# State-space layouts in DRAM, the products of the taps a step behind, and the rotary tables loaded earlier

## The chip, the core and the metric

The kernel runs on one core of a Trainium2 chip. The metric is device time in microseconds (us). Five engines run at the same time and are tied by semaphores: PE (matrix products; PEld, its weight load, lies beside it), DVE and ACT (element by element), POOL (here small additions, memsets and DMA issues) and SP (DMA issues only). Each engine takes its instructions in the order of the program.

## What is computed

The reference is a hybrid decoder block for one sequence of 512 rows, to which 16 learned rows are prepended (528 in all), width 2048. On the same RMS-normalised input run an attention with compressed queries and keys, and a diagonal complex state-space layer of 64 groups of 16 channels with 64 states each. The two are merged by gates; an output projection and a SwiGLU feed-forward layer follow.

```python
n = rms_norm(h, norm_mix[l])
z = n @ w_in[l]
q_lat, kv_lat, k_r, u, gates = jnp.split(z, [OFF_Q, OFF_KV, OFF_KR, OFF_U], axis=-1)
q = rms_norm(q_lat, norm_q[l]) @ w_q_up[l]          # 16 heads, 128 + 64 (rotary)
kv = rms_norm(kv_lat, norm_kv[l]) @ w_kv_up[l]
attn_out = mla_attention(q_nope, q_rope, k_nope, k_rope, v) @ w_attn_proj[l]
# state space: x_t = a x_(t-1) + b u_t,  y_t = Re(c x_t) + d u_t, per group
y = s5_scan(u.reshape(bsz, length, SSM_GROUPS, SSM_GROUP), lam_re, lam_im, log_step, b, c, d)
y = jax.nn.gelu(y)
ssm_out = (y @ w_glu_val[l]) * jax.nn.sigmoid(y @ w_glu_gate[l])
mixed = jax.nn.sigmoid(g0) * attn_out + jax.nn.sigmoid(g1) * ssm_out
h = h + mixed @ w_out[l]
h = h + (jax.nn.silu(m @ w_ffn_gate[l]) * (m @ w_ffn_up[l])) @ w_ffn_down[l]
out = rms_norm(h, norm_final)[:, N_META:]
```

## The kernel before

**Products and weights.** All is float32. A product with weights is made of three products of halves: weight and activation are each split into a high and a low half. Weights come in blocks of 8 tiles of 128 x 128 (512 KB). The class `Weights` streams them: SP loads a block into `raw`, ACT copies it to its high half `whi` (L262), DVE subtracts to get the low half `wlo` (L263), and a ring of three of each is kept ahead of PE. `st.use()` takes the next block. PE's instructions are nearly all at L316, inside `mm`; DVE's additions and products of two tiles are at L323 (`tt`), so groups are told apart by their tiles.

**Background work.** The program is written out by hand: the order of the calls is the order on each engine. Behind each block of weights a hook, `bg()`, lets generators in the background go on by a budget of time, at each of their `yield`s. So the work of the state-space layer is laid between the blocks of the projections: `ssm_first` beside the projections of u, q, kv (what the prediction calls the table stage), `ssm_main` and `x_products` beside the attention projection (the scan stage).

**The state-space layer.** The sequence is taken in 66 chunks (NC_) of 8 rows (CL), the 64 groups in four batches `b` of 16 groups (BG), a batch as 8 pairs (BP). u leaves the first projection transposed, one tile of 128 channels at a time: `evac_u` scales a tile on DVE and POOL stores it to `ud` (L871). `ssm_params` loads the parameters `sprm` (L519) and makes powers of the poles on DVE. Then, for each of the four batches, one after the other:

- `ssm_tables`: loads `sw` and `sK` (L669, L671); ACT copies C (through `C48`) and the first 18 columns of the powers `rt` into `ER`, DVE doubles these to 66 columns, POOL stores them to `ed` (L686). DVE expands the table BL in `ssA` (two halves of three operations of 128x1024). PE multiplies BL with C48 into the bank Q of the PSUM (psQ): these are the products of the tables, the taps of the filter; DVE adds them to `sK`, and eight stores of POOL take them to `kd` (L699). PE transposes BL in four groups (psB, L705), ACT copies them to `ssB` (L706), POOL stores that to `bd` (L708).
- `ssm_powers`: DVE expands the table CL, in the same tile `ssA` as BL, and four stores take it to `cd` (L720).

In `ssm_main` a batch loads BL's transposes (`load_b`, L743), its part of u (`load_u`, L737: eight loads, one for each row of a chunk, gathered in pieces of 264 bytes), the E tables (`load_e`, L748), and the matrix of taps (`load_t`): a memset of `ssB` (L763) and eight loads from `kd` (L766), which lay the taps as a block-Toeplitz matrix of 128 x 128 for each group, then CL (L770). PE makes the states' inputs, DVE scans, PE makes the outputs; `store` takes y to `yd` in eight stores (L823), from which the gates read it in rows of channels.

**Queues.** POOL issues these transfers in order. They take eight semaphores in turn, so that an issue waits for the transfer eight before it. What stands on POOL behind a waiting issue waits too.

**Rotary tables.** `kcs` (L933), the rotary table of the key, is loaded by POOL behind the last projection of kv; `cs` (L947), that of the queries, behind it, in the tile `sC`, which held C.

The loads of u and of the matrix of taps before:

```python
U = sb([P, BG, NC_], F32, ("U", "H0")[b % 2])
for i in range(CL):
    POOL.dma_start(U[i * 16:(i + 1) * 16],
                   ud[g0 * 16:(g0 + BG) * 16, CL - 1 - i].rearrange("(g p) c -> p g c", p=16))
```

## Time and profile before

| | before |
|---|---|
| time, median of 3 runs | 2859.46 us (2857.26 to 2861.65) |
| the profiled execution's own time | 2853.81 us |
| its span | 2852.0 us |
| mean granted clock of PE | 0.982 |
| PE busy | 2756.4 us, 97% of the span |
| PEld busy | 2601.1 us, 91% |
| DVE busy | 2047.4 us, 72% |
| ACT busy | 1222.1 us, 43% |
| POOL busy | 479.1 us, 17% |
| read from and written to DRAM | 342.32 MB and 75.10 MB, 146 GB/s over the span |

The span is the stretch between the first and the last instruction of the profiled execution; its own time has a little around it. The page gives the same busy shares in 40 slices of 71.3 us each, in tenths, and under them the clock granted to PE:

```profile
PE   9977999997899999999999999999999999999997
...
DVE  7866666655367777343468888888888888788896
...
POOL 2222211046420001111122000000000003030112
PEclk9988999998999999999999999999999999999999
DMA  5444222188664444544443433334333337474542
```

PE is below nine tenths in the third and fourth slices (143 to 285 us) and in the tenth and eleventh (642 to 784 us), and at the very end. Where PE waits, its clock is below full as well. The rows that the text below quotes from groups of instructions read: line, engine, operation, tile out <- tiles in, count, then busy us and mean ns of one, then the idle time before them and what ended most of it. Rows of the timeline begin with the time in us from the span's start and the duration, and end with the wait before them in brackets. Rows of stretches have the window, its length, then busy us and instructions of PE, PEld, DVE, ACT and POOL, then PE's granted clock, the busy share of the DMA engines, and GB/s.

### The profile page before, as it was taken

The numbers are of one execution on the slowest core, as the hardware profiler recorded it, in microseconds if no ns is written. First come the engines' busy times: TensorE is split into PE (matmuls) and PEld (weight loads), VectorE is DVE, ScalarE is ACT, GpSimd is POOL, SyncE is SP. The second block draws the span as 40 slices with busy tenths as digits, with TensorE's granted clock in tenths as the row PEclk, the third lists the DMA queues.
The fourth block names the chain that finished last, engine by engine and source line by source line (L and its number), as shares of the span: only waits on it lengthen the run. The fifth ranks groups of instructions, "written<-read, shape, count | busy, mean of one in ns | idle before, by whom it ended". The sixth has DMA issues, their size and how long they took to land.

```text
span 2852.0 us, 50236 instructions
## 1 busy us (share of the span) xinstructions
PE 2756.4 (97%) x20782; PEld 2601.1 (91%) x20782; DVE 2047.4 (72%) x2682; ACT 1222.1 (43%) x1774; POOL 479.1 (17%) x729
## 2 busy tenths in 40 slices
PE   9977999997899999999999999999999999999997
PEld 8876999976789999888889999999999999999997
DVE  7866666655367777343468888888888888788896
ACT  5222555532254445222234444444444445354445
POOL 2222211046420001111122000000000003030112
PEclk9988999998999999999999999999999999999999
DMA  5444222188664444544443433334333337474542
GB/s 190 143 130 119 82 67 67 49 243 260 190 251 148 137 150 143 162 138 144 135 138 126 148 126 126 133 134 141 127 133 129 138 127 258 162 266 157 196 166 97
DMA packets 126628, 426.38 MB, mean 149 GB/s; under 512 B 18208, under 2 KB 23008, under 8 KB 125312
## 3 DMA queue, kind: packets, MB, share of 16 engines
q1 hardware_dynamic: 76672, 263.36, 27.3%
q0 software_dynamic: 48944, 158.71, 17.3%
q8 instruction: 163, 2.67, 0.4%
q10 hardware_dynamic: 784, 1.11, 0.1%
q14 instruction: 65, 0.53, 0.1%
HBM read 342.32 MB, written 75.10 MB: 146 GB/s over the span
## 4 chain that ended last, share of the span: by engine, by line
PE 84%; DVE 6%; DMA 4%; issue 3%; POOL 1%; ACT 1%; DVEq 0%; POOLq 0%; ACTq 0%
PE psA L316 48%; PE psB L316 22%; PE psQ L316 6%; PE psV L316 5%; PE psD L316 2%; DVE T L323 1%; DMA ER<-ed 1%; DVE wlo L263 1%; DVE S L323 1%; DVE ev L323 1%; DMA xd<-H 1%; DMA sw<-in_sb 0%; ACT whi L262 0%; PE psA L1124 0%; PE psB L705 0%
## 5 line engine op out<-in xcount | busy, mean ns | idle before, releaser
L316 PE MATMUL psA<-S,whi 128*128 128x256 f32 (+2 forms) x5136 | 1122.9, 309 | 13.1 <-ACT whi L262 6.3
L316 PEld LDWEIGHTS psA<-S,whi 128*128 128x128 f32 x5136 | 843.7, 189 | 68.6 <-ACT whi L262 7.8
L316 PE MATMUL psA<-S,wlo 128*128 128x256 f32 (+2 forms) x2568 | 789.9, 308 | 0.0
L263 DVE TENSOR_TENSOR wlo<-raw,whi 128x1024 fp32r<-128x1024 f32 (+1 forms) x479 | 591.5, 1236 | 193.8 <-ACT whi L262 191.9
L262 ACT ACTIVATE whi<-raw 128x1024 fp32r<-128x1024 f32 (+1 forms) x479 | 504.5, 1055 | 414.8 <-PE psA L316 180.4
L316 PEld LDWEIGHTS psA<-S,wlo 128*128 128x128 f32 x2568 | 485.1, 189 | 26.0
L263 DVE TENSOR_TENSOR wlo<-cmb,whi 128x1024 fp32r<-128x1024 f32 x225 | 274.9, 1222 | 96.2 <-ACT whi L262 95.2
L316 PE MATMUL psB<-S,whi 128*128 128x256 f32 (+1 forms) x1632 | 330.1, 284 | 1.1 <-ACT ssB L706 0.9
L262 ACT ACTIVATE whi<-cmb 128x1024 fp32r<-128x1024 f32 x225 | 237.7, 1056 | 202.5 <-DVE wlo L263 142.0
L316 PEld LDWEIGHTS psB<-S,whi 128*128 128x128 f32 x1632 | 265.6, 190 | 2.4 <-ACT ssB L706 1.8
L316 PE MATMUL psB<-S,wlo 128*128 128x256 f32 (+1 forms) x816 | 230.3, 282 | 0.0
L316 PEld LDWEIGHTS psB<-S,wlo 128*128 128x128 f32 x816 | 154.6, 189 | 0.0
L1332 POOL DMA_DIRECT2D td<-sC x22 | 15.8, 718 | 764.4 <-ACT ev L1251 718.1
L316 PE MATMUL psA<-H,whi 128*128 128x512 f32 (+2 forms) x448 | 120.6, 356 | 11.4 <-DVE S L323 6.1
L316 PEld LDWEIGHTS psA<-H,whi 128*128 128x128 f32 x448 | 78.5, 194 | 22.3 <-issue 6.6
L243 DVE TENSOR_TENSOR cmb<-raw,raw 128x1024 f32<-128x1024 f32 x75 | 91.4, 1218 | 6.1 <-DMA raw<-in_wst 5.1
L323 DVE TENSOR_TENSOR H<-H,psA 128x256 f32<-128x256 f32 (+1 forms) x42 | 22.5, 535 | 96.8 <-POOL H L323 88.0
L243 DVE TENSOR_TENSOR cmb<-cmb,raw 128x1024 f32<-128x1024 f32 x75 | 91.4, 1219 | 0.0
L243 DVE TENSOR_TENSOR raw<-raw,raw 128x1024 f32<-128x1024 f32 x75 | 91.3, 1218 | 0.0
L243 DVE TENSOR_TENSOR cmb<-raw,cmb 128x1024 f32<-128x1024 f32 x75 | 91.3, 1217 | 0.0
L1251 ACT ACTIVATE ev<-psA 128x256 f32<-128x256 f32 x114 | 43.5, 381 | 100.8 <-PE psA L316 100.6
L316 PE MATMUL psA<-H,wlo 128*128 128x512 f32 (+2 forms) x224 | 78.3, 350 | 0.0
(675 smaller groups left out, 5461.7 us busy)
## 6 DMA issues: line engine op xcount, KB each, us to landing
raw<-in_wst SPq DMA_DIRECT2D x485, 512.0 KB, 3.7
td<-sC POOLq DMA_DIRECT2D x22, 512.0 KB, 3.2
td<-H POOLq DMA_DIRECT2D x40, 256.0 KB, 3.3
S<-td POOLq DMA_DIRECT2D x40, 256.0 KB, 7.1
H<-sg POOLq DMA_DIRECT2D x16, 512.0 KB, 4.0
bd<-ssB POOLq DMA_DIRECT2D x4, 1024.0 KB, 4.2
...
```

Source lines behind the costliest of these rows:

```text
L243: self.nc.vector.tensor_tensor(t, g(a), g(b), op=op)
L262: self.nc.scalar.activation(hi[:, a:b], w[:, a:b], AF.Copy)
L263: self.nc.vector.tensor_tensor(lo[:, a:b], w[:, a:b], hi[:, a:b], op=ALU.subtract)
L316: PE.matmul(o, lhsT=l, rhs=r, start=start, stop=stop, skip_group_check=more)
L323: eng.tensor_tensor(o, a, b, op=op)
L1251: ACT.activation(snap[name], o, AF.Copy)
L1332: POOL.dma_start(dst[0:2].rearrange("f p n -> p f n"), pair)
```

## The change

Five things are changed.

1. **u in DRAM.** `ud` is laid out as a batch takes it, [4, 128, 16, 66]. `evac_u` reverses the rows of a chunk and issues eight stores of 16 partitions (one for each group of the tile) instead of one; `load_u` is one load instead of eight.
2. **The matrix of taps in DRAM.** It is put together once, in the table stage, by a new function `toeplitz`, and stored whole to `wt` (1 MB for each batch); `load_t` is one load instead of a memset and eight loads.
3. **Order of the table stage.** `ssm_first` now holds the whole loop. CL is expanded right behind BL and has a tile of its own (the tag `ER`; the E tables went to `H7`). The products of the taps stand behind CL, go to the bank D, and are added and taken to `kd` a step later, by `toeplitz(*behind)`; the last one comes behind a `yield 5`. The powers `rt` lose their column of ones (17 instead of 18), C shares their tiles and is loaded earlier; CL is stored in two transfers instead of four.
4. **y in DRAM.** `store` is one store to `yt`; 32 copies from DRAM to DRAM (`y_rows`), four in each of eight tiles of the gates, lay the rows out in `yd`.
5. **Rotary tables.** `cs` is loaded before the projections of kv instead of behind them (its tile `sC` no longer holds C). `kcs` stays where it is.

```diff
-    ud = dp.tile([1024, CL, NC_], F32, name="ud")
+    ud = dp.tile([4, P, BG, NC_], F32, name="ud")
+    yt = dp.tile([4, P, BG, 64], F32, name="yt")
     yd = dp.tile([1024, CL, 64], F32, name="yd")
     kd = dp.tile([16, 64, CL, 16], F32, name="kd")
+    wt = dp.tile([4, P, BG * P], F32, name="wt")
...
         v = lambda t: t[:, :n_ * k].rearrange("p (a b) -> p a b", b=k)
-        bc = lambda t: t[:, :, m:m + 1].to_broadcast([P, n_, k])
-        cmul(e[0][:, :, m + 1:m + 1 + k], e[1][:, :, m + 1:m + 1 + k], e[0][:, :, 1:1 + k], e[1][:, :, 1:1 + k],
-             bc(e[0]), bc(e[1]), v(T1), v(T2))
+        bc = lambda t: t[:, :, m - 1:m].to_broadcast([P, n_, k])
+        cmul(e[0][:, :, m:m + k], e[1][:, :, m:m + k], e[0][:, :, :k], e[1][:, :, :k], bc(e[0]), bc(e[1]),
+             v(T1), v(T2))
...
-        rt = [sb([P, 32, 18], F32, t) for t in ("v", "w")]
-        tabs["rt"] = rt
-        POOL.memset(rt[0][:, :, 0], 1.0)
-        POOL.memset(rt[1][:, :, 0], 0.0)
+        vw = [sb([P, 2 * T], F32, t) for t in ("v", "w")]
+        rt = [t[:, :544].rearrange("p (j c) -> p j c", c=17) for t in vw]
+        C = [t[:, 544:].rearrange("p (j q) -> p j q", q=16) for t in vw]
+        tabs["rt"], tabs["C"] = rt, C
         for i in range(2):
-            DVE.tensor_copy(rt[i][:, :, 1], e8[:, i])
+            POOL.dma_start(C[i], A["sc"][:, i])
+            DVE.tensor_copy(rt[i][:, :, 0], e8[:, i])
         yield 0.4
         for m, k in ((1, 1), (2, 2), (4, 4), (8, 8), (16, 1)):
             double(rt, m, k, 32, T1, T2)
             yield 0.8 + 0.2 * k
 
-        C = sb([P, 2, 32, 16], F32, "sC")
-        tabs["C"] = C
-        POOL.dma_start(C, A["sc"])
         tabs["C48"] = sb([P, 2, BP, 48], F32, "U")
         POOL.memset(tabs["C48"], 0.0)
...
-    def ssm_tables(b):
...
-        ER = sb([P, 2, BP, NC_], F32, "ER")
-        for i in range(2):
-            ACT.activation(ER[:, i, :, :18], tabs["rt"][i][:, js], AF.Copy)
-        yield 0.3
-        for m, k in ((17, 17), (34, 31)):
-            double((ER[:, 0], ER[:, 1]), m, k, BP, T1, T2)
-            yield 1.0 + 0.05 * k
-        POOL.dma_start(ed[b], ER.rearrange("p a j c -> p a (j c)"))
-        BL = sb([P, 2, BP, CL * 16], F32, "ssA")
-        yield from expand(BL, Bt, js, 0, 1, T1, T2)
-        yield 1
-        pk = ps([P, 512], "Q")
-        for j in range(BP):
-            for i in range(2):
-                for r in RH:
-                    mm(pk[r, j * 32:(j + 1) * 32], BL[:, i, j, r], C48[:, i, j, 16:48], i == 0, i == 1)
-        tt(Dg, pk[:, :BG * 16], Dg, ADD)
-        for i in range(CL):
-            POOL.dma_start(kd[:, g0:g0 + BG, i], Dg[i * 16:(i + 1) * 16].rearrange("p (g o) -> p g o", o=16))
...
-    def ssm_powers(b):
-        js = slice(b * BP, (b + 1) * BP)
-        C48 = tabs["C48"]
-        CLt = sb([P, 2, BP, P], F32, "ssA")
-        yield from expand(CLt, C48, js, 1, -1, T1, T2)
-        for g in range(2):
-            for r in range(2):
-                POOL.dma_start(cd[b, g, r * 64:(r + 1) * 64],
-                               CLt[g * 64:(g + 1) * 64, r].rearrange("p j m -> p (j m)"))
-    def ssm_first():
-        yield from ssm_params()
-        for b in range(4):
-            yield from ssm_tables(b)
-            yield from ssm_powers(b)
+    def ssm_first():
...
+        def taps(b, BL):
+            pk = ps([P, 2, 512], "D")[:, 0]
+            for j in range(BP):
+                for i in range(2):
+                    for r in RH:
+                        mm(pk[r, j * 32:(j + 1) * 32], BL[:, i, j, r], C48[:, i, j, 16:48], i == 0, i == 1)
+            return pk
+        def transposed(b, BL, BT, j):
             pt = ps([P, 4, P], "B")
             for i in range(4):
                 PE.transpose(pt[:, i], BL[:, i % 2, j + i // 2], ident)
             ACT.activation(BT[:, j:j + 2].rearrange("p a b c -> p (a b) c"), pt, AF.Copy)
+        def toeplitz(b, pk, Dg):
             g0 = b * BG
+            tt(Dg, pk[:, :BG * 16], Dg, ADD)
             for i in range(CL):
+                POOL.dma_start(kd[:, g0:g0 + BG, i], Dg[i * 16:(i + 1) * 16].rearrange("p (g o) -> p g o", o=16))
             TT = sb([P, BG, P], F32, "ssB")
             POOL.memset(TT, 0.0)
             for i in range(CL):
                 s = CL - 1 - i
                 POOL.dma_start(TT[i * 16:(i + 1) * 16, :, s * 16:],
                                kd[:, g0:g0 + BG, 0:i + 1].rearrange("p g t o -> p g (t o)"))
+            POOL.dma_start(wt[b], TT.rearrange("p g m -> p (g m)"))
+        behind = None
+        for b in range(4):
+            js, g0 = slice(b * BP, (b + 1) * BP), b * BG
+            Bt = sb([P, 2, BP, 16], F32, "sw")
+            POOL.dma_start(Bt, A["sb"][:, :, js])
+            Dg = sb([P, BG * 16], F32, "sK", bufs=2)
+            POOL.dma_start(Dg, A["sd"][:, g0 * 16:(g0 + BG) * 16])
+            for ph, c in ((slice(0, P), 0), (RH[0], 16), (RH[1], 32)):
+                for i in range(2):
+                    ACT.activation(C48[ph, i, :, c:c + 16], tabs["C"][i][ph, js], AF.Copy)
+            ER = sb([P, 2, BP, NC_], F32, "H7")
+            POOL.memset(ER[:, 0, :, 0], 1.0)
+            POOL.memset(ER[:, 1, :, 0], 0.0)
+            for i in range(2):
+                ACT.activation(ER[:, i, :, 1:18], tabs["rt"][i][:, js], AF.Copy)
+            yield 0.1
+            for m, k in ((17, 17), (34, 31)):
+                double((ER[:, 0, :, 1:], ER[:, 1, :, 1:]), m, k, BP, T1, T2)
+                yield 1.0 + 0.05 * k
+            POOL.dma_start(ed[b], ER.rearrange("p a j c -> p a (j c)"))
+            if behind:
+                toeplitz(*behind)
+                yield 0.4
+            BL = sb([P, 2, BP, CL * 16], F32, "ssA")
+            yield from expand(BL, Bt, js, 0, 1, T1, T2)
+            CLt = sb([P, 2, BP, P], F32, "ER")
+            yield from expand(CLt, C48, js, 1, -1, T1, T2)
+            for g in range(2):
+                POOL.dma_start(cd[b, g].rearrange("(r s) m -> s r m", r=2),
+                               CLt[g * 64:(g + 1) * 64].rearrange("p r j m -> p r (j m)"))
+            behind = b, taps(b, BL), Dg
+            BT = sb([P, BP, 2, P], F32, "ssB")
+            for j in range(0, BP, 2):
+                transposed(b, BL, BT, j)
+                if j == 2:
+                    yield 0.1
+            POOL.dma_start(bd[b], BT.rearrange("p j a c -> p (j a c)"))
+            yield 0.1
+        yield 5
+        toeplitz(*behind)
...
         def load_u(b):
...
-            for i in range(CL):
-                POOL.dma_start(U[i * 16:(i + 1) * 16],
-                               ud[g0 * 16:(g0 + BG) * 16, CL - 1 - i].rearrange("(g p) c -> p g c", p=16))
+            POOL.dma_start(U, ud[b])
...
         def load_t(b):
             TT = sb([P, BG, P], F32, "ssB")
-            POOL.memset(TT, 0.0)
...
+            POOL.dma_start(TT.rearrange("p g m -> p (g m)"), wt[b])
...
         def store(b):
-            g0, Y = b * BG, nxt_["Y", b]
-            for t in range(CL):
-                POOL.dma_start(yd[g0 * 16:(g0 + BG) * 16, t].rearrange("(g p) c -> p g c", p=16),
-                               Y[t * 16:(t + 1) * 16])
+            POOL.dma_start(yt[b], nxt_["Y", b])
...
     def evac_u(j, outs):
         u = ev()
-        uv = u.rearrange("p (s c) -> p c s", s=CL)
+        uv = u.rearrange("p (s c) -> p c s", s=CL)[:, :, ::-1]
...
-        POOL.dma_start(ud[j * P:(j + 1) * P].rearrange("f s c -> f (s c)"), u)
+        rows = ud[j // 2].rearrange("(i p) g c -> p i g c", p=16)
+        for g in range(8):
+            POOL.dma_start(rows[:, :, j % 2 * 8 + g], u[g * 16:(g + 1) * 16].rearrange("p (i c) -> p i c", i=CL))
...
+    cs = sb([P, 2, SEQ], F32, "sC")
+    POOL.dma_start(cs, A["cs"][:, :, META:])
     acc_kv = sb([P, T], F32, "KS")
...
-    cs = sb([P, 2, SEQ], F32, "sC")
-    POOL.dma_start(cs, A["cs"][:, :, META:])
...
+    def y_rows(b, t):
+        POOL.dma_start(yd[b * BG * 16:(b + 1) * BG * 16, t].rearrange("(g p) c -> p g c", p=16),
+                       yt[b, t * 16:(t + 1) * 16])
...
+        for i in range(4 * j - 8, 4 * j - 4):
+            if 0 <= i < 32:
+                y_rows(i // CL, i % CL)
```

How the order of the instructions moves is shown at three places. A row is the line, the operation, the tile written and the tiles read (with a running number behind the name), and the shape; x8 stands for eight like rows. The lines of the changed kernel are its own.

First POOL near the start, while u is projected. `acc` is the sum of squares of the input, `ud` the stores of u, `sprm` the parameters with which the tables begin. Before:

```order
L323 TENSOR_TENSOR acc_112<-acc_112,ev_384 128x528
L871 DMA ud<-ev_567 128x528
L871 DMA ud<-ev_571 128x528
L871 DMA ud<-ev_575 128x528
L519 DMA sprm_635<-in_sprm 128x96
L871 DMA ud<-ev_726 128x528
```

And the same place with the change:

```order
L323 TENSOR_TENSOR acc_114<-acc_114,ev_386 128x528
L874 DMA ud<-ev_569 16x8x66 x8
L874 DMA ud<-ev_580 16x8x66 x8
L874 DMA ud<-ev_591 16x8x66 x8
L521 DMA sprm_658<-in_sprm 128x96
L874 DMA ud<-ev_749 16x8x66 x8
```

24 transfers instead of three stand ahead of the load of `sprm`.

Second DVE in the third step of the tables (b = 2), where the projection of q ends. `T` and `T_..` are the two terms of an expansion, `ssA` BL, `ev` and `psQ` the norm of q, `wlo` a block of weights. Before, from the first half of BL on:

```order
L323 TENSOR_TENSOR T_132_1857<-sw_1853,spw_184 128x1024
L323 TENSOR_TENSOR T_133_1858<-sw_1853,spw_184 128x1024
L323 TENSOR_TENSOR ssA_1932<-T_132_1857,T_133_1858 128x1024
L332 TENSOR_SCALAR ev_1936<-psQ_1937 128x512
L323 TENSOR_TENSOR ev_1936<-ev_1936,acc_1307 128x512 x2
L332 TENSOR_SCALAR ev_1936<-ev_1936 128x512
L323 TENSOR_TENSOR acc_1307<-acc_1307,ev_1936 128x512
```

With the change, from the second half of BL on (`ER` is CL here, `U` holds C48):

```order
L323 TENSOR_TENSOR T_83_1352<-sw_1849,spw_186 128x1024
L323 TENSOR_TENSOR T_84_1353<-sw_1849,spw_186 128x1024
L323 TENSOR_TENSOR ssA_1961<-T_83_1352,T_84_1353 128x1024
L263 TENSOR_TENSOR wlo_1969<-raw_1729,whi_1968 128x1024
L323 TENSOR_TENSOR T_83_1352<-U_1289,spw_186 128x1024
L323 TENSOR_TENSOR T_84_1353<-U_1289,spw_186 128x1024
L323 TENSOR_TENSOR ER_2022<-T_83_1352,T_84_1353 128x1024
L332 TENSOR_SCALAR ev_2026<-psQ_2027 128x512
```

The norm of q stood between the two halves of BL, ahead of the products; it now stands behind BL and the first half of CL.

Third POOL at the end of the tables (b = 3), up to the load of `kcs` (tile `S`). `KS` is the sum of squares of kv. Before:

```order
L699 DMA kd<-sK_2222 16x16x16 x8
L708 DMA bd<-ssB_2469 128x2048
L323 TENSOR_TENSOR KS_1792<-KS_1792,ev_2504 128x528
L720 DMA cd<-ssA_2497 64x1024 x4
L933 DMA S_196_2656<-in_kcs 128x528
L938 DMA KS_2661<-S_196_2656 64x528
L947 DMA sC_2669<-in_cs 128x2x512
```

With the change, behind `bd` and the addition to `KS`:

```order
L690 DMA kd<-sK_2225 16x16x16 x8
L692 MEMSET ssB_2671 128x2048
L695 DMA ssB_2671<-kd 16x16x16
L695 DMA ssB_2671<-kd 16x16x32
L695 DMA ssB_2671<-kd 16x16x48
L695 DMA ssB_2671<-kd 16x16x64
L695 DMA ssB_2671<-kd 16x16x80
L695 DMA ssB_2671<-kd 16x16x96
L695 DMA ssB_2671<-kd 16x16x112
L695 DMA ssB_2671<-kd 16x2048
L697 DMA wt<-ssB_2671 128x2048
L938 DMA S_186_2756<-in_kcs 128x528
```

The stores to `kd`, the memset, the eight loads of the matrix and its store now stand right ahead of the load of `kcs`.

More of the change, by code (lines that the diff above doesn't have):

```diff
@@ L627, in ssm_params @@
             yield 0.8 + 0.2 * k
-        C = sb([P, 2, 32, 16], F32, "sC")
-        tabs["C"] = C
-        POOL.dma_start(C, A["sc"])
         tabs["C48"] = sb([P, 2, BP, 48], F32, "U")
         POOL.memset(tabs["C48"], 0.0)
-        yield 3.6
         cfb = lambda i: cf[:, i].unsqueeze(2).to_broadcast([P, 32, 16])
         c1, c2, c3 = (t.rearrange("p (a b) -> p a b", b=16) for t in (T1[:, :512], T1[:, 512:1024], T2[:, :512]))
-        tt(c1, C[:, 0], cfb(0), MUL)
-        tt(c2, C[:, 1], cfb(1), MUL)
+        tt(c1, C[0], cfb(0), MUL)
+        tt(c2, C[1], cfb(1), MUL)
         tt(c1, c1, c2, SUB)
-        tt(c2, C[:, 0], cfb(1), MUL)
+        tt(c2, C[0], cfb(1), MUL)
         yield 2.8
-        tt(c3, C[:, 1], cfb(0), MUL)
-        stt(C[:, 1], c2, -1.0, c3, MUL, SUB)
-        DVE.tensor_copy(C[:, 0], c1)
+        tt(c3, C[1], cfb(0), MUL)
+        stt(C[1], c2, -1.0, c3, MUL, SUB)
+        DVE.tensor_copy(C[0], c1)
         yield 2.1
@@ L662, in expand @@
         yield 3.7
-    def ssm_tables(b):
-        js, g0 = slice(b * BP, (b + 1) * BP), b * BG
-        Bt = sb([P, 2, BP, 16], F32, "sw")
-        POOL.dma_start(Bt, A["sb"][:, :, js])
-        Dg = sb([P, BG * 16], F32, "sK")
-        POOL.dma_start(Dg, A["sd"][:, g0 * 16:(g0 + BG) * 16])
+    def ssm_first():
+        yield from ssm_params()
         T1 = sb([P, 2 * T], F32, "T1")
         T2 = sb([P, 2 * T], F32, "T2")
-        C, C48 = tabs["C"], tabs["C48"]
-        for ph, c in ((slice(0, P), 0), (RH[0], 16), (RH[1], 32)):
-            ACT.activation(C48[ph, :, :, c:c + 16], C[ph, :, js], AF.Copy)
-        ER = sb([P, 2, BP, NC_], F32, "ER")
-        for i in range(2):
-            ACT.activation(ER[:, i, :, :18], tabs["rt"][i][:, js], AF.Copy)
-        yield 0.3
-        for m, k in ((17, 17), (34, 31)):
-            double((ER[:, 0], ER[:, 1]), m, k, BP, T1, T2)
-            yield 1.0 + 0.05 * k
-        POOL.dma_start(ed[b], ER.rearrange("p a j c -> p a (j c)"))
-        BL = sb([P, 2, BP, CL * 16], F32, "ssA")
-        yield from expand(BL, Bt, js, 0, 1, T1, T2)
-        yield 1
-        pk = ps([P, 512], "Q")
-        for j in range(BP):
-            for i in range(2):
-                for r in RH:
-                    mm(pk[r, j * 32:(j + 1) * 32], BL[:, i, j, r], C48[:, i, j, 16:48], i == 0, i == 1)
-        tt(Dg, pk[:, :BG * 16], Dg, ADD)
-        for i in range(CL):
-            POOL.dma_start(kd[:, g0:g0 + BG, i], Dg[i * 16:(i + 1) * 16].rearrange("p (g o) -> p g o", o=16))
-        yield 0.4
-        BT = sb([P, BP, 2, P], F32, "ssB")
-        for j in range(0, BP, 2):
+        C48 = tabs["C48"]
+        def taps(b, BL):
[6 more added lines that the diff above has]
+        def transposed(b, BL, BT, j):
             pt = ps([P, 4, P], "B")
@@ L723, in ssm_first @@
-    def ssm_first():
-        yield from ssm_params()
-        for b in range(4):
-            yield from ssm_tables(b)
-            yield from ssm_powers(b)
+        def toeplitz(b, pk, Dg):
+            g0 = b * BG
+            tt(Dg, pk[:, :BG * 16], Dg, ADD)
+            for i in range(CL):
+                POOL.dma_start(kd[:, g0:g0 + BG, i], Dg[i * 16:(i + 1) * 16].rearrange("p (g o) -> p g o", o=16))
+            TT = sb([P, BG, P], F32, "ssB")
+            POOL.memset(TT, 0.0)
+            for i in range(CL):
+                s = CL - 1 - i
+                POOL.dma_start(TT[i * 16:(i + 1) * 16, :, s * 16:],
+                               kd[:, g0:g0 + BG, 0:i + 1].rearrange("p g t o -> p g (t o)"))
+            POOL.dma_start(wt[b], TT.rearrange("p g m -> p (g m)"))
@@ L733, in load_u @@
         def load_u(b):
-            g0 = b * BG
             U = sb([P, BG, NC_], F32, ("U", "H0")[b % 2])
-            for i in range(CL):
-                POOL.dma_start(U[i * 16:(i + 1) * 16],
-                               ud[g0 * 16:(g0 + BG) * 16, CL - 1 - i].rearrange("(g p) c -> p g c", p=16))
+            POOL.dma_start(U, ud[b])
             nxt_["U", b] = U
@@ L759, in load_t @@
         def load_t(b):
-            g0 = b * BG
             TT = sb([P, BG, P], F32, "ssB")
-            POOL.memset(TT, 0.0)
-            for i in range(CL):
-                s = CL - 1 - i
-                POOL.dma_start(TT[i * 16:(i + 1) * 16, :, s * 16:],
-                               kd[:, g0:g0 + BG, 0:i + 1].rearrange("p g t o -> p g (t o)"))
+            POOL.dma_start(TT.rearrange("p g m -> p (g m)"), wt[b])
             C2 = [sb([P, BP, P], F32, t) for t in ("H2", "H3")]
```

3 lines of the change are left out of this document (removed).

## The prediction

> **What bounds the kernel now.** The page's shares come first: PE is busy 97% of the span, DVE 72%, DMA less, so only stretches in which PE waits can give time. The second view is PE's waits by releaser, once for 60 to 320 us (from here the table stage: the state-space tables are made in the background of the projections) and once for 560 to 800 us (the scan stage, beside the attention projection). Columns: total us, times, longest.
>
> ```profile
> PE psQ L316 <- DVE ssA L323: 16.5, 5, 8.0
> PE psA L316 <- DVE S L323: 6.1, 1, 6.1
> PE psB L705 <- ACT ssB L706: 4.6, 8, 0.7
> ...
> PE psD L316 <- DMA U<-ud: 8.9, 1, 8.9
> PE psD L316 <- DMA ao<-sC: 8.1, 1, 8.1
> PE psV L316 <- DMA ssB<-kd: 3.9, 1, 3.9
> PE psD L316 <- DMA H<-ud: 3.6, 1, 3.6
> ```
>
> The products of the taps (psQ) wait 16.5 us for DVE's table BL, and the scan stage waits 24.5 us for transfers, with 1.9 more put down to issue. (The 8.1 named ao<-sC stands at a product that reads U, whose load then lands.) Third, the stretches around these waits, with PE's busy time and, after the POOL column, its granted clock:
>
> ```profile
> 145.00:165.00 20.00, 16.09 (x118) 13.20 (x118) 13.04 (x12) 3.75 (x6) 5.78 (x9) 0.83 0.33 103
> 189.00:213.00 24.00, 13.49 (x118) 11.67 (x117) 15.17 (x19) 7.78 (x11) 6.90 (x11) 0.64 0.33 95
> 232.00:254.00 22.00, 15.02 (x125) 13.20 (x124) 12.38 (x12) 4.98 (x8) 7.50 (x12) 0.69 0.43 123
> ...
> 623.00:635.00 12.00, 8.35 (x67) 6.92 (x64) 4.83 (x9) 4.99 (x6) 6.82 (x12) 0.72 0.84 252
> 660.00:687.00 27.00, 12.24 (x121) 10.32 (x120) 8.74 (x13) 4.65 (x7) 15.07 (x27) 0.68 0.94 284
> 715.00:731.00 16.00, 7.89 (x110) 6.90 (x110) 4.39 (x5) 3.61 (x5) 4.22 (x9) 0.79 0.65 200
> ```
>
> A wait costs twice: behind it PE runs slowly for some us. Busy time times the missing clock is 2.7 + 4.9 + 4.7 = 12 us in the first three, and 2.3 + 3.9 + 1.7 = 8 us in the last three. So about 34 us can be had in the table stage (16.5 + 4.6 + 12, and 0.9 of small waits) and 34 in the scan stage (26.4 + 8). Elsewhere the change meets a busy PE.
>
> **Term 1, the start: +7 us.** Each evacuation of U now issues 8 stores instead of 1, and three evacuations come at once, ahead of the load of sprm on POOL.
>
> ```profile
> 40.59 5.79 PE psD L316 x48
> ...
> 46.92 0.56 POOL L871 DMA_DIRECT2D ud<-ev  x1 [10.81 <-DVE ev L323]
> 49.45 0.54 POOL L519 DMA_DIRECT2D sprm<-in_sprm  x1
> ...
> 53.50 0.18 DVE L332 TENSOR_SCALAR sw<-sprm 128x32 f32<-128x32 f32 x1 [3.83 <-DMA sprm<-in_sprm]
> 56.82 1.23 DVE L263 TENSOR_TENSOR wlo<-raw,whi 128x1024 fp32r<-128x1024 f32 x1
> ```
>
> 24 stores at 0.56 from 46.92 put sprm's issue at 60.4. It landed 4.05 us after its issue, so DVE starts at 64.4, not 53.5, and the wlo behind its chain ends at 68.9, not 58.0. That wlo belongs to the tenth weight block. PE ended the sixth at 46.4 and takes 5.8 for each, so it reaches the tenth at 63.8 and the first matmul with wlo at 64.3: a wait of 4.6. The slow clock behind it I take as 2.4, by the row 145:165 (waits of 3.7, loss 2.7). Ends: 0, if DVE's slack covers it after all, and +12.
>
> The Trainium skill (TensorE: Matmul & The Clock Gate, Part 1) states that the clock halves after an idle window of about 3.4 us and returns after a busy one as long. By that rule the loss here is an estimated 1.7 and waits under 3.4 us lose nothing; the stretch 145:165, whose longest wait is 3.25, shows a loss, so I keep the measured 2.4; the sum would be 0.7 lower by the rule.
>
> **Term 2, the table stage: -14 us.** Products now stand behind the whole of CL in the program, two weight blocks after BL, and CL has a tile of its own. So the psQ waits go, and DVE decides. Its time from 105 to 255 us, and its largest waits (last column; these for 105 to 265):
>
> ```profile
> 105.00:255.00 150.00, 127.91 (x946) 113.45 (x946) 108.64 (x145) 39.76 (x66) 42.89 (x68) 0.87 0.45 138
> ...
> L263 DVE TENSOR_TENSOR wlo<-raw,whi 128x1024 fp32r<-128x1024 f32 x18 | 23.9, 1326 | 13.3 <-ACT whi L262 13.3
> L323 DVE TENSOR_TENSOR ssA<-T,T 128x1024 f32<-128x1024 f32 x16 | 19.6, 1225 | 13.5 <-PE psB L705 13.0
> L323 DVE TENSOR_TENSOR T<-sw,spw 128x1024 f32<-128x1024 f32 x16 | 18.9, 1219 | 4.3 <-DMA sw<-in_sb 4.1
> ```
>
> DVE works 108.6 of 150 and idles 41.4. Gone: 13.0 (CL no longer waits for the transposes), 4.1 (sw has the time of the E tables to land), 2.5 of the add to sK (its product is a step old), and about 6 of the 13.3, which are DVE ahead of PE. New: in three steps ACT copies C48 and the E tables behind the transposes' copies, so DVE starts a step about 4 us late: +12. That makes 108.6 + 27.8 = 136.4, and the block that ended at 255 ends near 241: -14. PE's own floor is 127.9 - 12.3, so it doesn't bind. The last word at step 2 is still DVE's: ACT copies the transposes behind the second normalised piece of q, so PE's wait of 8 moves from the products to the third transpose.
>
> The rest is the chain of toeplitz, which now stands on POOL within this stage:
>
> ```profile
> L699 POOL DMA_DIRECT2D kd<-sK x32 | 18.0, 570 | 44.6 <-DVE sK L323 44.6
> kd<-sK POOLq DMA_DIRECT2D x32, 16.0 KB, 1.9
> bd<-ssB POOLq DMA_DIRECT2D x4, 1024.0 KB, 4.2
> ...
> 601.16 1.84 POOL L763 MEMSET ssB<- 128x2048 f32 x1
> 603.30 4.46 POOL L766 DMA_DIRECT2D ssB<-kd  x8 [0.29 <-POOL ssB L763]
> ssB<-kd POOLq DMA_DIRECT2D x4, 128.0 KB, 5.4
> ```
>
> Eight stores 4.5, memset 1.8 and 0.3, eight loads 4.5, the last to land about 3.5 more (5.4 where the transfers are crowded), and wt, 1 MB like bd, 4.2: 19 us from the add to a free ssB. From the add to the step's transposes DVE has BL, CL (7.1 each, from six operations of 1.2), two wlo and an evacuation, about 18. So ACT waits 1 to 3 us in steps 1 and 3, in my 241. Ends of this term: -30 (PE's floor) and +5.
>
> **Term 3, the end of the table stage: +3 us.** The early rotary tables take away DVE's wait of 3.6, but POOL loads kcs behind the last toeplitz:
>
> ```profile
> 255.64 0.43 DVE L332 TENSOR_SCALAR ev<-psQ 128x264 f32<-128x264 f32 x1 [3.50 <-PE psQ L316]
> 265.37 0.58 POOL L933 DMA_DIRECT2D S<-in_kcs  x1
> 273.79 0.71 DVE L323 TENSOR_TENSOR S<-S 128x528 f32<-128x528 f32 x1
> 280.01 1.29 DVE L323 TENSOR_TENSOR ev<-psA,sC 128x512 f32<-128x512 f32 x2 [3.62 <-DMA sC<-in_cs]
> 281.36 0.81 PE L316 MATMUL psA<-H,whi 128*128 128x264 f32 x2 [4.82 <-DVE ev L323]
> ```
>
> In before's times: that chain starts on DVE at 255.6, so sK's add is done at 260.3; stores, memset and loads have landed by 274.5, wt is issued, kcs follows at 275 and lands behind wt's megabyte near 281. The product with kcs, 273.8 before, starts there; behind it on DVE are one wlo and the rotary products, on which PE waits: 284 against 281.4. Ends: -9 and +6.
>
> **Term 4, the scan stage: -24 us.**
>
> ```profile
> 585.00:735.00 150.00, 123.49 (x995) 100.92 (x995) 74.79 (x102) 34.53 (x46) 74.36 (x124) 0.90 0.83 258
> 635.00:640.00 5.00, 5.00 (x106) 4.31 (x105) 2.88 (x5) 1.00 (x2) 0.10 (x1) 1.00 1.02 413
> ...
> 612.34 0.72 POOL L748 DMA_DIRECT2D ER<-ed  x1
> 623.23 0.56 POOL L737 DMA_DIRECT2D H<-ud  x1 [1.70 <-DMA ER<-ed]
> ACT ER L757 <- DMA ER<-ed: 36.9, 4, 16.4
> ```
>
> Per batch 8 + 8 + 8 POOL transfers and a memset become 3 transfers: 21 x 0.56 + 1.8 = 14 us less on POOL. The eighth piece of U, held at 623.23 until the E table of 612.34 had landed (the program lets eight POOL transfers be under way), becomes one load right behind E. What is late next is bandwidth: 258 GB/s x 150 us is 39 MB, and whole toeplitz tiles (1 MB for 0.6) make it 40. Without its 34 us PE leaves 116 us for them: 345 GB/s, 84% of the 413 of the best row. While x_products run beside it, bursts must bind, so I leave 10 us of waiting: -24. Ends: -34 and -8.
>
> **Nothing elsewhere.** The 32 small copies from yt to yd cost POOL 18 us over eight tiles of the gates, where PE is full and POOL nearly idle:
>
> ```profile
> 900.00:950.00 50.00, 50.00 (x426) 50.00 (x426) 36.85 (x39) 23.48 (x30) 2.57 (x4) 1.00 0.46 150
> ```
>
> Without that cover (a late load of ao) it would be a few us. The 17th table column and the earlier load of C move a wait of 1.8.
>
> **Sum.** +7 - 14 + 3 - 24 = -28. The profiled execution took 2853.81 (span 2852.0, 1.8 around it), which lies 5.65 under the median of the three runs, 2859.46; so 2826 for its like, and 2832 as a median.
>
> **Rivals.** (a) The toeplitz chain is much longer than 19 us. Each us more delays ACT's copies in steps 1 and 3 and kcs, three places (step 2 is covered); from 28 us on all gain is gone, and at 31, with slow clock, it ends slower: 2832 + 36 + 4 = 2872. For it: 128 KB took 5.4 under load, and POOL waits in order. Against: quiet stores landed in 1.9. Chance 0.07. (b) The small stores do not overlap: 24 x 1.9 instead of 24 x 0.56 is 32 us more before sprm, and PE waits for it: 2864. Against: eight kd stores were issued 0.57 apart. The Trainium skill (DMA: Bandwidth & Descriptors, Rules for kernel authors) says that transfers under 64 KB pay mostly overhead, which speaks for this; chance 0.02. (c) The scan stage stays bound by its transfers, for the same bytes and more pass while x_products run (0.94 busy at 660:687): only 8 us gained, 2848. Chance 0.18. (d) All goes well: products and transposes never wait (-26) and the scan stage loses its 34: 2810. Chance 0.17. (e) The products still wait, since DVE is only shifted: term 2 is 0, 2846; 0.06.
>
> **How the numbers follow.** The forecast has 0.5, its own range 2815 to 2845. With (c), (d), (e) the range 2809 to 2853 holds 8 in 10. About 0.2% (5.7 us) is what a measurement can tell from no change: faster 0.84 (forecast, d, and nearly all of c and e), same 0.08, slower 0.08 (a, b).
>
> **What would show it.** Term 1: DVE's first sprm row near 64 with a wait of about 14, and a PE wait near 64. Term 2: no psQ or psD row with DVE ssA, but psB L683 <- ACT ssB of several us at the third step. Term 3: a DVE wait for in_kcs of about 9 us, none for in_cs. Term 4: PE's waits on U and H<-ud under 10 us in all, and no row of POOL held by ER<-ed. Wrong would be: ACT waiting long on ssB<-wt in every step (a), or PE idle as before at 660 to 730 (c).

## The result and the profile after

| | before | after |
|---|---|---|
| time, median of 4 runs | 2858.36 us (2854.26 to 2861.65) | 2837.41 us (2837.18 to 2837.92) |
| ratio | 1 | 0.9928, 95% interval 0.991 to 0.9945 |
| profiled execution: time, span | 2853.81, 2852.0 us | 2837.2, 2835.4 us |
| mean granted clock of PE | 0.982 | 0.986 |
| POOL busy | 479.1 us | 496.1 us |

The change makes the kernel 0.72% faster, which is 20.6 us of the median of before (15.7 to 25.7). Between the two profiled executions it is 16.6 us, since that of before lies 4.6 us under its median and that of after at its median.

PE's waits by releaser in the first 1000 us of after (total us, times, longest):

```profile
PE psB L683 <- ACT ssB L684: 17.0, 5, 10.4
PE psA L316 <- DVE ev L323: 11.3, 1, 11.3
PE psA L316 <- DVE wlo L263: 8.8, 4, 2.9
PE psB L683 <- DVE H L323: 7.5, 1, 7.5
...
PE psV L316 <- DMA H<-v: 3.6, 1, 3.6
PE psA L316 <- DVE S L323: 3.0, 1, 3.0
PE psD L316 <- DMA U<-ud: 1.3, 1, 1.3
```

The waits of the products (psQ) are gone, but the table stage now waits in other places, and for longer. The waits of the scan stage shrank from 26.4 to 4.9 us. The same stretches as before say so too (window, length, PE, PEld, DVE, ACT, POOL, clock, DMA, GB/s):

```profile
105.00:255.00 150.00, 119.76 (x913) 106.38 (x912) 115.76 (x156) 36.93 (x72) 64.66 (x108) 0.88 0.57 166
...
585.00:735.00 150.00, 143.65 (x1156) 117.16 (x1155) 96.60 (x129) 48.62 (x70) 41.49 (x73) 0.98 0.83 304
660.00:687.00 27.00, 22.08 (x215) 18.12 (x215) 16.44 (x24) 6.38 (x9) 8.71 (x15) 0.87 0.98 355
```

PE's 127.91 us of 150 in the table stage fell to 119.76. In the scan stage 123.49 rose to 143.65, POOL's 74.36 fell to 41.49, and the transfers moved 304 GB/s instead of 258. From 660 to 687 us, where PE had worked 12.24 us, it works 22.08.

A second measure serves for all that follows. ACT makes a copy `whi` of each block of weights, in the same order in every kernel here. The start of such a copy minus the start of the same copy in before tells how far a kernel is behind (+) or ahead (-) at that place. The columns are copies that start in before at 98.8 us (the tables begin), 257.2 (their last step), 294.5 (the attention begins) and 770.1 (the gates); the fifth is the fourth minus the third, the gain of the scan stage, and the last the span less 2852.0. Behind the number of an experiment stands the kernel that it is built on.

| kernel | 98.8 | 257.2 | 294.5 | 770.1 | scan stage | span |
|---|---|---|---|---|---|---|
| after | +3.5 | +10.5 | +14.6 | -14.3 | -28.9 | -16.6 |
| E1: after, sprm first | +1.0 | +3.2 | +7.2 | -21.7 | -28.9 | -24.1 |
| E2: after, matrix in load_t | +3.9 | +2.7 | -4.4 | -23.8 | -19.4 | -27.3 |
| E3: E2, products behind BL | +4.6 | +1.6 | -5.6 | -23.6 | -18.0 | -25.1 |
| E4: before, u alone | +4.2 | +16.0 | +15.5 | +7.9 | -7.6 | +5.4 |
| E5: after, y in eight stores | +4.4 | +11.1 | +15.1 | -3.8 | -18.9 | -5.5 |
| E6: after, sprm and kcs early | +0.3 | +3.9 | +3.7 | -24.6 | -28.3 | -27.5 |
| E7: E2, sprm first | 0.0 | -4.9 | -12.0 | -29.3 | -17.3 | -31.4 |
| E8: E7, products between CL's halves | +1.1 | -9.8 | -16.7 | -34.4 | -17.7 | -35.9 |
| E9: E7, half of CL | +1.2 | -13.3 | -21.1 | -36.0 | -14.9 | -37.2 |
| E10: E8, matrix from DRAM to DRAM | +0.6 | +2.3 | -4.8 | -33.5 | -28.7 | -33.5 |
| E11: E10, zeros spread | +0.7 | -8.1 | -14.3 | -43.4 | -29.1 | -45.8 |

The changed kernel thus lost 14.6 us up to the attention, where the prediction had a gain of 4, and won 28.9 in the scan stage, where it had 24. E1 to E10 are one run each, and every row comes from one trace. How far such rows agree is seen where kernels have the same code: the five with sprm behind the 24 stores lie from +3.5 to +4.6 at 98.8, and the scan stages with single transfers of u and y and the matrix in `load_t` (E2, E3, E7, E8, E9) from -14.9 to -19.4. The last 2.3 us of the span lie behind 770.1; in the twelve rows that rest is between 0 and 3.5 us, in E4 too, which has none of the change there, so it is not read.

### The profile page after: what moved, and what is told of

Same layout as the page of the kernel before. It is cut to its first block, busy times and chain, and to the rows that moved or that the text cites. A ratio compares the mean times of both kernels' runs of the same rounds, so it can differ in the third digit from the quotient of the medians.

```text
span 2835.4 us, 50272 instructions
## 1 busy us (share of the span) xinstructions
PE 2747.7 (97%) x20782; PEld 2593.5 (91%) x20782; DVE 2049.9 (72%) x2682; ACT 1222.6 (43%) x1786; POOL 496.1 (17%) x768
## 3 DMA queue, kind: packets, MB, share of 16 engines
q1 hardware_dynamic: 76672, 263.36, 27.1%
## 4 chain that ended last, share of the span: by engine, by line
PE 81%; DVE 6%; DMA 3%; issue 2%; POOL 1%; ACT 1%; DVEq 0%; ACTq 0%; POOLq 0%
PE psA L316 48%; PE psB L316 20%; PE psQ L316 6%; PE psV L316 5%; PE psD L316 1%; DVE wlo L263 1%; DVE S L323 1%; DVE T L323 1%; DVE ev L323 1%; DMA U<-ud 0%; DMA ER<-td 0%; PE psA L1127 0%; DMA ssB<-kd 0%; DMA T<-td 0%; DVE cmb L243 0%
## 5 line engine op out<-in xcount | busy, mean ns | idle before, releaser
L316 PEld LDWEIGHTS psA<-S,wlo 128*128 128x128 f32 x2568 | 485.5, 189 | 35.9 <-DVE wlo L263 10.4
L316 PE MATMUL psA<-H,whi 128*128 128x512 f32 (+2 forms) x448 | 120.3, 356 | 15.1 <-DVE ev L323 11.3
L1254 ACT ACTIVATE ev<-psA 128x256 f32<-128x256 f32 x114 | 43.4, 381 | 100.6 <-PE psA L316 100.6
```

What stands on the lines that cost most here:

```text
L316: PE.matmul(o, lhsT=l, rhs=r, start=start, stop=stop, skip_group_check=more)
L1254: ACT.activation(snap[name], o, AF.Copy)
```

## The experiments

**E1, sprm first.** Is the loss at the start that of the load behind 24 stores?

```diff
+    tabs = {"prm": sb([P, 3, 32], F32, "sprm")}
+    POOL.dma_start(tabs["prm"], A["sprm"])
...
     def ssm_params():
-        prm = sb([P, 3, 32], F32, "sprm")
-        POOL.dma_start(prm, A["sprm"])
+        prm = tabs["prm"]
```

> Changed kernel, but the load of sprm is issued by POOL before the stores of u instead of behind 24 of them. Theory: the start lost 3.3 us because DVE, in order, waited 13.2 us for sprm and a wlo stood behind it; here DVE does not wait, PE's waits for wlo near 68 us are gone, and every later block is 3.3 us earlier than in the changed kernel (span about 2832). Rival: the tables only begin earlier and then wait for the same blocks, so that blocks 14 to 18 are earlier but the table stage ends where it did (span 2835).

The timeline of DVE in after, and of PE in after, at the place in question:

```profile
63.18 0.18 DVE L332 TENSOR_SCALAR sw<-sprm 128x32 f32<-128x32 f32 x1 [13.21 <-DMA sprm<-in_sprm]
66.50 1.23 DVE L263 TENSOR_TENSOR wlo<-raw,whi 128x1024 fp32r<-128x1024 f32 x1
...
67.78 0.39 PE L316 MATMUL psA<-S,wlo 128*128 128x264 f32 x1 [2.79 <-DVE wlo L263]
```

With sprm first, DVE begins the powers at 50.61 without a wait, and PE does not wait. Both theories fell short: of the 7.4 us that E1 is ahead of after at 294.5, about 2.5 come at the start, and the rest in the tables (+3.5 to +10.5 in after, +1.0 to +3.2 here). A late start is paid a second time there, since DVE begins 12.6 us later than in E1 but PE is only 2.5 behind; DVE's work on the powers then reaches into the tables. In after PE waits once more for wlo in the first step and then runs at a slower clock; E1 has no wait there, and its clock from 120 to 130 us is 1.00.

```profile
127.65 0.63 PE L316 MATMUL psA<-S,wlo 128*128 128x512 f32 x1 [2.40 <-DVE wlo L263]
...
127.00:136.00 9.00, 8.35 (x74) 6.73 (x74) 7.32 (x8) 2.53 (x3) 0.00 (x0) 0.81 0.24 68
```

Wait and slow clock (8.35 us times the missing 0.19) make 4.0 of the 4.8 us that after loses more than E1 in the tables.

**E2, the matrix in load_t.** What did the matrix in the table stage cost and bring?

```diff
         def toeplitz(b, pk, Dg):
...
-            TT = sb([P, BG, P], F32, "ssB")
-            POOL.memset(TT, 0.0)
-            for i in range(CL):
...
-            POOL.dma_start(wt[b], TT.rearrange("p g m -> p (g m)"))
...
         def load_t(b):
             TT = sb([P, BG, P], F32, "ssB")
-            POOL.dma_start(TT.rearrange("p g m -> p (g m)"), wt[b])
+            POOL.memset(TT, 0.0)
+            for i in range(CL):
...
```

> Changed kernel, but the matrix of taps is put together in load_t again (memset and eight loads from kd), so that nothing but the eight stores to kd stands behind sK's addition, and no wt. Theory A (the chain to wt holds ACT's copies of the transposes and kcs): PE's wait of 5.0 us at the second step of the tables goes, the one of 7.5 at the fourth shrinks by less than 2, since DVE is late there too, the 10.4 at the third stays; PE's wait of 11.3 us near 295 falls to about 5. The block near 300 us is 11 to 15 us earlier than in the changed kernel. Theory B (DVE's own work sets the table stage): up to 265 us within 2 us of the changed kernel. Scan stage: if the gain there is the single load of u, it keeps at least 20 of the 29 us gained; if it is the matrix, it keeps under 12.

The chain in after, in step 1, on POOL, then ACT and PE behind it; then ACT and PE in step 3, and DVE at kcs:

```profile
149.90 4.50 POOL L690 DMA_DIRECT2D kd<-sK  x8 [1.20 <-DVE sK L323]
154.40 1.83 POOL L692 MEMSET ssB<- 128x2048 f32 x1
156.52 4.38 POOL L695 DMA_DIRECT2D ssB<-kd  x8 [0.29 <-POOL ssB L692]
166.77 0.59 POOL L697 DMA_DIRECT2D wt<-ssB  x1 [5.87 <-DMA ssB<-kd]
...
172.97 1.08 ACT L684 ACTIVATE ssB<-psB 128x512 f32<-128x512 f32 x2 [7.48 <-DMA wt<-ssB]
...
173.62 1.97 PE L683 MATMUL psB<-ident,ssA 128*128 128x128 f32 x8 [4.98 <-ACT ssB L684]
...
256.30 1.23 ACT L684 ACTIVATE ssB<-psB 128x512 f32<-128x512 f32 x2 [7.33 <-DMA wt<-ssB]
...
255.78 3.13 PE L683 MATMUL psB<-ident,ssA 128*128 128x128 f32 x12 [7.50 <-DVE H L323]
...
291.63 0.71 DVE L323 TENSOR_TENSOR S<-S 128x528 f32<-128x528 f32 x1 [10.53 <-DMA S<-in_kcs]
```

Without it the wait of 5.0 at step 1 falls to 0.25, that of 7.5 at step 3 to 1.2 (I expected it to stay, since DVE seemed late there too; the profile puts it down to DVE, but it goes with the chain), and that of 11.3 at kcs to 2.4; the 10.4 at step 2 stays, 10.8. E2 is ahead of after by 7.8 us at 257.2 and by 19.0 at 294.5, more than expected. It gives back 9.5 us in the scan stage. So the matrix in `wt`, put together in this place, cost about twice what it brought.

**E3, the old place of the products.** On E2: products and transposes right behind BL, ahead of CL.

```diff
             yield from expand(BL, Bt, js, 0, 1, T1, T2)
-            CLt = sb([P, 2, BP, P], F32, "ER")
-            yield from expand(CLt, C48, js, 1, -1, T1, T2)
...
             POOL.dma_start(bd[b], BT.rearrange("p j a c -> p (j a c)"))
             yield 0.1
+            CLt = sb([P, 2, BP, P], F32, "ER")
+            yield from expand(CLt, C48, js, 1, -1, T1, T2)
...
```

> As the kernel with the matrix in load_t, but products and transposes stand right behind BL again, ahead of CL, which keeps a tile of its own. The prediction's view (products behind CL free PE of 16.5 us of waits): this kernel's PE waits for ssA come back, about 16 us, and its block near 260 us is at least 8 us later than with the matrix in load_t alone. Rival (the wait only moved from the products to the transposes, and CL's own tile is what helps DVE): waits of PE in the table stage within 4 us of each other, and the block near 260 us within 4 us.

PE's waits from 40 to 320 us, of E2 and then of E3:

```profile
PE psB L682 <- ACT ssB L683: 15.2, 8, 10.8
PE psA L316 <- DVE wlo L263: 9.8, 5, 4.6
```

```profile
PE psD L316 <- DVE ssA L323: 19.8, 6, 8.3
PE psB L682 <- ACT ssB L683: 4.4, 7, 0.7
PE psA L316 <- DVE wlo L263: 2.6, 1, 2.6
```

25.0 against 26.8 us, and 1.1 us between the two kernels at 257.2: the rival holds. Two blocks behind BL, the products wait no more, and the transposes and the blocks of weights wait in their stead.

**E4, u alone,** on the kernel before (its layout, stores and load as in the change's diff).

> The kernel before with only the layout of u changed: eight stores of each tile, one load for each batch. Theory: the start loses 3.3 us as in the changed kernel; the table stage is that of before; in the scan stage the waits on U and H<-ud (8.9 + 8.1 + 3.6 us) and most of the slow clock behind them go, 18 to 24 us; span 2831 to 2838. Rival: the matrix of taps with its memset and eight loads is late in their place, PE's waits for ssB<-kd grow from 3.9 to over 12, and under 12 us are gained.

The scan stage gains 7.6 us, and U and H<-ud still wait 12.9 us; ssB<-kd waits 5.4, so the matrix is not what took their place. The start loses 4.2 us, but the table stage does not stay that of before: PE waits 24.1 us for ssA instead of 16.5, and the kernel is 16.0 behind at 257.2. In the order before, a start that is 4.2 us late costs almost three times as much again.

**E5, y in eight stores,** on after, with `store` as before and no `y_rows`.

> Changed kernel, but y goes from store to yd in eight stores for each batch again, and no rows are copied beside the gates. The scan stage gained 28.9 us in the changed kernel; 9.5 of it goes with the matrix (the run with the matrix in load_t kept 19.4) and 7.7 with u alone. Theory: the rest, about 12 us, is the one store of y, which frees POOL of seven issues ahead of the next batch's loads: here the scan stage gains only 15 to 19 us, span 2845 to 2849. Rival: the parts are not additive, and y is worth under 4 us: span under 2840.

The scan stage gains 18.9 us instead of 28.9, as forecast. With E2 and E4 the gain has three sources of like size: matrix 9.5, y 10.0, u 7.6; together 27.1 of 28.9. (By the spread of like scan stages above, each is good to a few us; E10 against E8 gives 11.0 for the matrix.) What eight stores do to POOL is seen in before (its timeline): they take it from 645.74 to 652.57, since three of them wait for older transfers (of xd), and the next batch's loads stand behind.

```profile
645.74 2.83 POOL L823 DMA_DIRECT2D yd<-H  x5
649.71 0.56 POOL L823 DMA_DIRECT2D yd<-H  x1 [1.14 <-DMA xd<-H]
650.62 0.56 POOL L823 DMA_DIRECT2D yd<-H  x1 [0.35 <-DMA xd<-H]
652.02 0.56 POOL L823 DMA_DIRECT2D yd<-H  x1 [0.84 <-DMA xd<-H]
```

**E6, sprm and kcs early,** with the matrix in `wt`; kcs goes to another tile, ahead of the last projection's blocks.

```diff
+    kcs = sb([P, T], F32, "v")
+    POOL.dma_start(kcs, A["kcs"])
     o = halves("A", "B")
...
-    POOL.dma_start(krc[:, 1], A["kcs"])
```

> Changed kernel with the matrix kept in the table stage, but sprm loaded ahead of the stores of u, and kcs loaded (into another tile) ahead of the last projection's blocks instead of behind the last chain to wt. Theory: 7.4 us at the start and in the tables, as in the run with sprm first, and 9 to 11 us at kcs, as in the run with the matrix in load_t: PE's wait of 11.3 us near 290 falls to under 3, span 2816 to 2820. Rival: behind kcs PE waits for something else of the last chain, and under 5 us of it are gained: span over 2822.

The rival: only 3.5 us are gained at kcs (E1 +7.2, here +3.7). POOL has one more transfer behind the last chain, krs, and DVE now waits for that one. PE's wait of 11.3 us becomes one of 1.1 and one of 5.5 (timelines of POOL and DVE in E6):

```profile
279.50 0.59 POOL L697 DMA_DIRECT2D wt<-ssB  x1 [3.97 <-DVE acc L323]
281.67 0.55 POOL L944 DMA_DIRECT2D KS<-S  x1 [1.58 <-issue]
...
284.46 0.70 DVE L323 TENSOR_TENSOR S<-S,KS 64x528 f32<-64x528 f32 x1 [4.95 <-DMA KS<-S]
```

**E7, E2 with sprm first.**

> Matrix in load_t and sprm loaded ahead of the stores of u. If a late start of the tables costs the same as in the changed kernel, 7.4 us less than with the matrix in load_t alone, span 2817; if the 4 us that it had over come from the chain to wt, only the direct 3 to 4 us, span 2821.

At 294.5 it is 7.6 us ahead of E2, as E1 was of after: what a late start costs in the tables does not come from the chain to wt. The scan stage gains 2.1 us less than in E2, which is within the spread of this code, and the span, 2820.6, lies nearer to the second forecast.

**E8, products between the halves of CL,** on E7: one block of weights behind BL.

```diff
+            half = expand(CLt, C48, js, 1, -1, T1, T2)
+            yield next(half)
             behind = b, taps(b, BL), Dg
...
+            yield from half
```

> As the run with the matrix in load_t and sprm first, but the products and the transposes stand between the two halves of CL, one block of weights behind BL instead of two. Theory 1 (the copies of the transposes wait behind work on DVE and ACT that they do not need): the wait of 10.8 us at the third step falls under 4, no wait for ssA over 2 us comes in its place, and the block near 300 us is 6 to 10 us earlier than in its base. Theory 2 (DVE's work in order sets the stage, and PE waits for it wherever the products stand): waits only change their place, and that block is within 2.5 us.

At step 2 the wait of 9.8 us falls to 1.9 and 4.0 (timelines of PE, E7 and then E8):

```profile
202.90 1.12 PE L682 MATMUL psB<-ident,ssA 128*128 128x128 f32 x4 [9.83 <-ACT ssB L683]
```

```profile
185.71 0.66 PE L682 MATMUL psB<-ident,ssA 128*128 128x128 f32 x4 [1.94 <-DVE H L323]
190.40 1.11 PE L682 MATMUL psB<-ident,ssA 128*128 128x128 f32 x4 [4.03 <-ACT ssB L683]
...
226.02 1.11 PE L682 MATMUL psB<-ident,ssA 128*128 128x128 f32 x4 [4.83 <-DVE H L323]
```

but one of 4.8 comes at the last step. It is 4.7 us ahead of E7 at 294.5, between the two theories.

**E9, half of CL,** on E7. The second half of CL is not computed; POOL sets it to zero.

```diff
-            yield from expand(CLt, C48, js, 1, -1, T1, T2)
+            POOL.memset(CLt[:, 1], 0.0)
+            yield next(expand(CLt, C48, js, 1, -1, T1, T2))
+            yield 3.7
```

> As the run with the matrix in load_t and sprm first, but the second half of CL is not computed: POOL sets it to zero, so DVE has three operations of 1.2 us less in each of the four steps, 14.6 us in all. Theory 1 (the prediction's: DVE's work is the sum that sets the table stage): the block near 260 us is 11 to 15 us earlier than in that base. Theory 2 (a step is a chain through ACT, DVE and PE in which the transposes two blocks behind BL and ACT's copies behind them decide): under 6 us earlier, and DVE only idles more.

8.4 us ahead of E7 at 257.2 (9.6 from 98.8 on) for 14.6 us of DVE's work, again between the theories. DVE then idles more, above all for ACT's copies of the E tables: 17.0 us instead of 10.0. DVE's sum counts, but only somewhat more than half of it.

**E10, the matrix from DRAM to DRAM,** on E8. It was not to pass through ssB, nor stand ahead of kcs.

```diff
+            for i in range(CL):
+                s = CL - 1 - i
+                POOL.dma_start(wt[b, i * 16:(i + 1) * 16].rearrange("p (g m) -> p g m", m=P)[:, :, s * 16:],
+                               kd[:, g0:g0 + BG, 0:i + 1].rearrange("p g t o -> p g (t o)"))
...
+        zero = sb([P, BG * P], F32, "ssB")
+        POOL.memset(zero, 0.0)
+        for b in range(4):
+            POOL.dma_start(wt[b], zero)
```

> As the run with products and transposes between the halves of CL, but the matrix of taps is laid out in wt in the table stage by eight copies from DRAM to DRAM for each batch (those of the last batch behind krs), on a ground of zeros stored once; ssB takes no part, and load_t is one load. Theory (the matrix in wt is worth 9.5 us in the scan stage, and cost time in the table stage only because ACT's copies and kcs stood behind its chain): table stage within 2 us of its base, scan stage 8 to 10 us shorter, span 2806 to 2810. Rival: POOL's issues and the copies' small pieces delay the table stage by as much, span over 2813.

By the span the rival, but not by its cause. The scan stage gained 28.7 us, as with the matrix in `wt`, and the table stage lost 12.1 against E8 by 257.2, most of it in the first step, where DVE waits for sw (DVE's timeline in E10, and the line on sw's landing):

```profile
121.33 2.36 DVE L323 TENSOR_TENSOR T<-sw,spw 128x1024 f32<-128x1024 f32 x2 [8.75 <-DMA sw<-in_sb]
...
DMA to landing us min/median/max: 14.7/14.7/14.7
```

POOL issued it at 106.51, right behind the 4 MB of zeros.

**E11, the zeros in two pairs** between the stores of u, where sw is not yet loaded.

```diff
-        yield from ssm_params()
...
+        for i, cost in enumerate(ssm_params()):
+            if 1 <= i < 5:
+                POOL.dma_start(wt[i - 1], zero)
+            yield cost
```

> As the run whose matrix is laid out from DRAM to DRAM, but the four stores of zeros (1 MB each) are issued in two pairs between the stores of u at 60 to 90 us instead of together right ahead of the load of sw. Theory (in that run the load of sw lay behind 4 MB of zeros, DVE began BL 11 us late, and nothing else was wrong with the copies): the table stage is that of the run with products between the halves (block near 300 us 15 to 18 us ahead of the kernel before), the scan stage keeps its 27 us: span 2805 to 2811. Rival: the zeros delay the stream of weights or the copies the table stage in their new place too: span over 2815.

The theory held: 14.3 us ahead of before at 294.5 (a little less than forecast), a scan stage of -29.1, span 2806.2. Over five rounds the median is 2809.5 us (2808.11 to 2812.51) against 2856.65 of the kernel before, ratio 0.9838, 95% interval 0.9825 to 0.9852. This version beats both kernels: the changed kernel's median, in other rounds, was 2837.41.

## Why the prediction was right in the total and wrong in the tables

The time, 2837.41 us, lies 5 us over the forecast of 2832 and in the range. The nearness is in part luck. The forecast added 5.65 us because the profiled execution of before lay below its median; that of after lay at its median, so the change itself was forecast at 28 us and measured 16.6 between the profiled executions. And errors of opposite sign met: the table stage came out 21 us worse than forecast, the start and the scan stage 4 and 5 better.

**Term 1** (+7): +3.2 at its place (from +0.3 before 63 us to +3.5). DVE began at 63.18 (64.4 forecast), and PE's wait was 2.79 instead of 4.6, since sprm landed 2.1 us after its issue, not 4.05, and PE came later. Behind it PE ran at full clock, so the 2.4 us of slow clock were not there:

```profile
60.00:68.00 8.00, 5.21 (x43) 5.00 (x42) 4.30 (x19) 1.06 (x1) 1.61 (x3) 1.00 0.16 23
68.00:72.00 4.00, 4.00 (x35) 4.00 (x35) 3.34 (x18) 0.00 (x0) 0.00 (x0) 1.00 0.38 135
...
159.00:162.00 3.00, 3.00 (x8) 2.32 (x9) 2.97 (x3) 0.00 (x0) 1.90 (x4) 0.50 0.93 257
```

The Trainium skill (TensorE: Matmul & The Clock Gate, Part 1) states that the clock halves after an idle window of about 3.4 us. Read as in the prediction, that a shorter wait loses nothing, it agrees with the first two rows; it does not agree with the third, in which the clock is 0.50 behind a wait of 2.85 us. What the term left out is larger: the 4 to 5 us that the late start costs again in the tables (E1, E7).

**Term 2** (-14) is the step that failed: +7.0 (+3.5 to +10.5). The sum took DVE as what sets the stage, left its work as it was and let its idle time fall by 13.6 us (41.4 to 27.8 of its window). Neither came. Between the copies at 98.8 and 257.2, with the same 1011 products on PE, the stretches are these (before, then after):

```profile
98.76:257.17 158.41, 136.32 (x1011) 121.69 (x1010) 112.83 (x151) 41.83 (x69) 42.89 (x68) 0.88 0.46 140
```

```profile
102.25:267.71 165.46, 134.39 (x1011) 120.47 (x1010) 121.88 (x165) 42.41 (x81) 67.34 (x110) 0.88 0.58 170
```

DVE works 9.1 us more (3.6 of it with the late start: 118.3 in E1; where all the rest comes from was not followed) and idles 43.6 us instead of 45.6. DVE's largest waits, 105 to 265 us, in after:

```profile
DVE wlo L263 <- ACT whi L262: 17.0, 8, 5.3
DVE T L323 <- ACT H L714: 16.1, 4, 6.8
DVE H L320 <- ACT H L319: 2.8, 4, 0.7
```

The waits for the transposes, for sw and for sK are gone or small, as forecast. But the wait for whi, which was to shrink by 6, grew from 13.3 to 17.0, and that for the E tables is 16.1 instead of 12. This looks like a loop of PE, ACT and DVE in which each waits for the next; what is shown is that work taken from DVE counts somewhat over half (E9). Of the 21 us between forecast and result, the late start explains 4 to 5 (E1: 10.5 - 3.5 against 3.2 - 1.0; E7 against E2: 3.7). The chain of toeplitz explains about 8 (E2): it took 23.8 us from sK's addition at 149.19 to ACT's copy at 172.97, not 19, as its last load landed 5.2 us behind the issues instead of 3.5, and `wt` took 6.1 us to land instead of 4.2. The working allowed 1 to 3 us of ACT's time in each of two steps; ACT waited 7.48 and 7.33. The rest, about 9, is E7's -4.9 against -14: with neither fault the reorder brings only that, and E8 wins about half of the rest, by placing the products one block behind BL instead of two. By the same stretches DVE idles 37.5 us in E7 and 31.6 in E8: only there does the idle time fall by the forecast amount. Why the remaining few us stay is open. The forecast wait of 8 at the third transpose was there, with 10.4. E3 shows that the new place of the products by itself is worth nothing.

**Term 3** (+3): +4.1, by the forecast mechanism. DVE waited 10.53 us for kcs and not at all for cs. Its working priced the transfer alone; E6 shows that krs, behind the same chain, keeps about half of PE's wait even with kcs loaded early.

**Term 4** (-24): -28.9, the mechanism right. No issue of POOL waits for the E table any more. The 10 us left for bandwidth were too many: PE waited 4.9, and the transfers went at 304 GB/s over 585:735. The prediction counted POOL's transfers as one sum; that the gain is spread about evenly over matrix, y and u (E2, E4, E5) was not worked out in it. The copies of y beside the gates cost nothing, as forecast: after is 14.3 us ahead at 770.1, and still at the copy that starts in before at 1272 us.

**Rivals.** Rival (a) occurred at a smaller dose: 24 us instead of 28 of chain do not take the whole gain, but E2, without it, is 19.0 us ahead at 294.5. Rival (b) did not occur: sprm landed before 63.18, and 24 stores at 1.9 each would have put it near 97. Rival (c) did not occur: PE works 22.08 of the 27 us from 660 on. Rival (e) describes the table stage better than the forecast did, though not by its letter: the products no longer wait, but by E3 their wait only moved to the transposes and the weights.
